# A two-layer diffusion block in split fp32 products: modulation sums, gates and an accumulator's first term moved between VectorE and ScalarE

## The chip, the cores and the metric

The kernel runs on one NeuronCore of a Trainium2 chip. A core has engines that run side by side, each with its own queue of instructions: TensorE (PE, the matrix products; its weight loads are shown apart as PEld), VectorE (DVE), ScalarE (ACT), GpSimd (POOL) and SyncE (SP, which starts transfers). They meet through semaphores. Matrix products leave their sums in PSUM, which VectorE and ScalarE can read and write; everything else lies in SBUF. The metric is the device time of one execution in microseconds (us), the median over runs.

## The reference

All is computed in fp32, on 256 latent tokens (`lat`) and 256 context tokens (`cx`) of width 1024. Layer 0 mixes by a short convolution, layer 1 by attention; after layer 1's mixer only the latent tokens are needed. Cut to what is computed here:

```python
def _rms(t, g):
    y = t * lax.rsqrt(jnp.mean(t * t, axis=-1, keepdims=True) + 1e-6)
    return y * g
def _modulate(t, g, shift, scale):
    return _rms(t, g) * (1 + scale) + shift
def _swiglu(h, w13, w2):                      # w13: 1024 x 5632, w2: 2816 x 1024
    gte, up = jnp.split(h @ w13, 2, axis=-1)
    return (jax.nn.silu(gte) * up) @ w2

for i in range(2):
    mod  = (silu(c)     @ mod_w[i] + mod_b[i]).reshape(bsz, 3, 3, 1, 1024)
    modc = (silu(c_ctx) @ mod_w[i] + mod_b[i]).reshape(3, 3, 1024)
    lat = lat + 0.5 * mod[:, 0, 2] * _swiglu(_modulate(lat, norm_g[i, 0], mod[:, 0, 0], mod[:, 0, 1]),
                                             ffn_w13[i, 0], ffn_w2[i, 0])
    cx  = ...                                 # the same with modc
    h, hc = _modulate(lat, norm_g[i, 1], ...), _modulate(cx, norm_g[i, 1], ...)
    y, yc = short_conv(h), short_conv(hc)     # i = 0: (b * dwconv3(c * x)) @ w_out
    y, yc = attention(h, hc), None            # i = 1: 8 query heads, 2 key heads, rope
    lat = lat + mod[:, 1, 2] * y
    if i == 0: cx = ...                       # mixer and second swiglu for cx too
    lat = lat + 0.5 * mod[:, 2, 2] * _swiglu(_modulate(lat, norm_g[i, 2], ...), ffn_w13[i, 1], ffn_w2[i, 1])
return lat
```

## The kernel before

**Products.** An fp32 product is three products of split operands: a high half (a ScalarE copy, L98) and the rest (a VectorE subtraction, L99), hi x hi + hi x lo + lo x hi (`mm3`, L118). Every weight is loaded raw (`wr`, three buffers of 128 x 2048), split (`split`, tiles `wh` and `wl`) and used. Names with h or l at the end (`gh`, `bl`, `th`) are such halves of activations. Tokens are the moving side: 256 (`S`, one stream) or 512 (`T2`, both).

**Swiglu.** `ffn(l, b, ...)` (L611) takes the 22 tiles of 128 hidden units in thirds of 8, 7 and 7. Each third makes its gated tiles g, and `project` (L462) multiplies them by w2 into 8 output tiles, which `finish` (L441) scales by the gate vector and adds to x, by one VectorE operation for each stream (L446). Most hidden tiles are computed by `Pair` (L539 on): the 2x2 block product (two halves of the model width by two streams, gate and up weights as the other side) in 7 products of half size in place of 8. A pair forms sums of weight blocks S1 to S4 (VectorE, into `ws`, L557 to L567), and uses sums T1 to T4 of the normed activations (`sums`, L320, one per normed block set). Its products are A11, A12, S1, S2, S4, S3, A22, twelve matmuls of 256 columns each, in two PSUM banks p and q. `head` does A11 into p and A12 into q's first half, `five` S1, `six` S2 and S4, `seven` S3, `four` A22; `seven` and `four` of a pair are placed among the next pair's products, or between the first products of `project`. The gate is copied out of p (L585, L595), added to q on VectorE (L597), and put through Silu (L598).

In ffn(0,0) tiles 3 to 7 of the first third are plain products. In ffn(0,1) and ffn(1,0) the first third starts with two plain tiles whose two streams are done one after the other, while the norm of the second stream is still being made; `Blocks.block` (L296) norms 4 x 256 columns at a time (VectorE products t with the rms factor, L256, ScalarE affine steps L305 and L310, then a split), and the T sums and the first pair's weight sums are made there too.

**Modulation.** The vectors `mod` are dot products of weight rows with silu(c): 224 units of one VectorE instruction each with an accumulated sum (`mod_unit`, L142) and a read-out of the accumulator. `tick(n)` (L179) spreads them over the program: a call adds n to what is owed, and each whole unit owed is issued. `mod_ready` (L186) issues the rest of a vector when it is needed.

**Attention and the last swiglu.** Heads are done in a loop: `scores` (L1033; maximum on VectorE, exponential on ScalarE, the scaling `pn` on POOL, L1058), `turn` (transposes, L1067, and a split) and `mix`. The last swiglu (from L1162, latent tokens only) does its first four tiles by `first_mm` on columns that need no norm yet (258 wide) and divides later (`first_post`, L1194). Tile 1 of them is followed by the norm of all 8 blocks of x: per block one VectorE product, one ScalarE high half (L1226) and one VectorE low half (L1227). The other tiles use matmuls of 512 and 256 columns (`mm2`, L1107).

**What sets the order.** The program is written in one order, and a scheduler places every instruction in its engine's queue by the dependencies it sees and its own estimate of when they are ready; an engine then runs its queue strictly in order. Six PSUM banks are shared by all products (`psum`, in rotation), two more serve small ones.

## Time and profile before

| | |
|---|---|
| median of 3 runs | 1587.94 us (1587.75 to 1588.68) |
| profiled execution | 1589.78 us, its span 1588.0 us |
| mean granted TensorE clock | 0.995 |
| TensorE busy | 1565.0 us, 99% |
| VectorE busy | 1319.8 us, 83% |
| ScalarE busy | 738.2 us, 46% |
| GpSimd busy | 29.8 us, 2% |
| read from HBM | 244.77 MB, 155 GB/s over the span |

Rows of the profile have the form "line engine operation output<-inputs, partitions x elements, x count". In a group's row the first number behind the bar is the busy time of the group in us, the next the mean of one in ns, and behind the second bar stands the idle time of the engine just before these instructions and what ended it. In a row of the timeline the first number is the start in us from the span's start, the second the busy time; an idle time before it stands in brackets. In a row of stretches the numbers are start and end, length, then busy time and instructions of PE, PEld, DVE, ACT and POOL, the granted clock of TensorE (1 is full speed), the busy share of the DMA engines, and GB/s. Matmuls overlap, so their pitch is read from start to start, not from the duration of one. A row of waits has "instruction <- releaser: us in total, times, longest us".

### The profile page before, as it was taken

The page shows a single profiled execution, that of the slowest core. Times are in us where ns is not written, and L with a number is a line of the kernel's source. Part 1 is how long each engine was busy: PE and PEld are TensorE (multiplying, and loading weights), DVE is VectorE, ACT ScalarE, POOL GpSimd, SP SyncE. Part 2 cuts the span into 40 slices and gives each one's busy share as a digit, 9 for nine tenths or more (in the row PEclk, how much of TensorE's full clock was granted, in tenths as well). Part 3 has the DMA queues.
Part 4 walks back from the last instruction along what each step waited for, and adds up shares of the span by engine and source line. Part 5 has one row for each costly group of instructions (what it writes and reads, how often), then busy time and mean ns, then how long its engine had stood idle before and what let it go on. Part 6 is the DMA issues. An engine that isn't in the chain of part 4 may idle for free.

```text
span 1588.0 us, 25040 instructions
## 1 busy us (share of the span) xinstructions
PE 1565.0 (99%) x10210; PEld 1423.9 (90%) x10210; DVE 1319.8 (83%) x2029; ACT 738.2 (46%) x1180; POOL 29.8 (2%) x20
## 2 busy tenths in 40 slices
PE   8999999999999999999999999999999999899998
PEld 6788998998888899989899899899899898888887
DVE  5778778879998879799798899898898899976654
ACT  5532452544322356335345375335255455655543
POOL 0000000000000000000000000000000005200000
PEclk9999999999999999999999999999999999999999
DMA  8545234234565412452342423443433654645552
GB/s 319 181 174 201 92 115 167 104 117 162 186 214 193 177 65 95 142 200 104 130 177 102 160 103 107 158 161 107 175 133 122 235 186 149 234 156 186 186 202 90
DMA packets 38419, 248.74 MB, mean 157 GB/s; under 512 B 5280, under 2 KB 7072, under 8 KB 11936
## 3 DMA queue, kind: packets, MB, share of 16 engines
q1 hardware_dynamic: 35712, 245.38, 43.5%
q10 hardware_dynamic: 2592, 1.76, 0.4%
q8 instruction: 80, 1.31, 0.3%
q14 instruction: 35, 0.29, 0.1%
HBM read 244.77 MB, written 1.05 MB: 155 GB/s over the span
## 4 chain that ended last, share of the span: by engine, by line
PE 93%; DVE 3%; ACT 2%; DMA 1%; issue 1%; POOL 0%; DVEq 0%; POOLq 0%; ACTq 0%
PE py L122 9%; PE py L123 9%; PE py L124 9%; PE p L124 7%; PE p L123 7%; PE p L122 7%; PE q L122 5%; PE q L123 5%; PE q L124 5%; PE py L1107 3%; PE pg L1107 2%; PE pu L1107 2%; PE pg L122 2%; PE pg L123 1%; PE pg L124 1%; PE pu L124 1%
## 5 line engine op out<-in xcount | busy, mean ns | idle before, releaser
L98 ACT ACTIVATE wh<-wr 128x1024 fp32r<-128x1024 f32 (+2 forms) x276 | 277.2, 1015 | 352.2 <-PE py L123 81.2
L99 DVE TENSOR_TENSOR wl<-wr,wh 128x1024 fp32r<-128x1024 f32 (+2 forms) x276 | 319.7, 1166 | 78.4 <-ACT wh L98 71.0
L142 DVE CUSTOM_DVE_ANT_0 junk<-wr,scbc,modb 128x1024 bf16<-128x1024 f32 x224 | 286.8, 1280 | 25.0 <-DMA wr<-in_modT 22.2
L123 PE MATMUL py<-gl,wh 128*128 128x512 f32 (+1 forms) x570 | 213.3, 374 | 0.0
L122 PE MATMUL py<-gh,wh 128*128 128x512 f32 (+1 forms) x570 | 213.3, 374 | 0.0
L124 PE MATMUL py<-gh,wl 128*128 128x512 f32 (+1 forms) x570 | 213.0, 374 | 0.0
L99 DVE TENSOR_TENSOR wl<-ws,wh 128x1024 fp32r<-128x1024 f32 x108 | 131.3, 1223 | 28.6 <-ACT wh L98 28.1
L98 ACT ACTIVATE wh<-ws 128x1024 fp32r<-128x1024 f32 x108 | 113.4, 1058 | 75.1 <-DVE ws L563 32.5
L124 PEld LDWEIGHTS py<-gh,wl 128*128 128x128 f32 x570 | 107.3, 188 | 19.1
L122 PEld LDWEIGHTS py<-gh,wh 128*128 128x128 f32 x570 | 107.4, 188 | 18.5
L123 PEld LDWEIGHTS py<-gl,wh 128*128 128x128 f32 x570 | 107.4, 188 | 18.2
L123 PE MATMUL p<-tl,wh 128*128 128x256 f32 x432 | 122.2, 283 | 0.0
L124 PE MATMUL p<-th,wl 128*128 128x256 f32 x432 | 122.2, 283 | 0.0
L122 PE MATMUL p<-th,wh 128*128 128x256 f32 x432 | 122.2, 283 | 0.0
L122 PE MATMUL q<-bh,wh 128*128 128x256 f32 x320 | 90.6, 283 | 0.0
L123 PE MATMUL q<-bl,wh 128*128 128x256 f32 x320 | 90.6, 283 | 0.0
L124 PE MATMUL q<-bh,wl 128*128 128x256 f32 x320 | 90.6, 283 | 0.0
L122 PEld LDWEIGHTS p<-th,wh 128*128 128x128 f32 x432 | 82.9, 192 | 0.3
L123 PEld LDWEIGHTS p<-tl,wh 128*128 128x128 f32 x432 | 82.9, 192 | 0.3
L124 PEld LDWEIGHTS p<-th,wl 128*128 128x128 f32 x432 | 82.9, 192 | 0.0
L446 DVE SCALAR_TENSOR_TENSOR x<-py,G,x 128x256 f32<-128x256 f32 x144 | 62.9, 477 | 6.3 <-PE py L124 6.0
L557 DVE TENSOR_TENSOR ws<-wr 128x1024 f32<-128x1024 f32 x54 | 65.7, 1218 | 0.0
(296 smaller groups left out, 4181.1 us busy)
## 6 DMA issues: line engine op xcount, KB each, us to landing
wr<-in_w SPq DMA_DIRECT2D x88, 1024.0 KB, 4.9
wr<-in_modT SPq DMA_DIRECT2D x64, 1024.0 KB, 4.8
wr<-in_w2b SPq DMA_DIRECT2D x24, 896.0 KB, 4.6
wr<-in_w2a SPq DMA_DIRECT2D x12, 1024.0 KB, 4.8
wr<-in_mod SPq DMA_DIRECT2D x8, 1024.0 KB, 6.1
wr<-in_cw_cx SPq DMA_DIRECT2D x8, 1024.0 KB, 4.8
wr<-in_w2l SPq DMA_DIRECT2D x8, 1024.0 KB, 4.8
wr<-in_cw_b SPq DMA_DIRECT2D x4, 1024.0 KB, 4.9
```

The lines of the kernel that those rows point to most:

```text
L98: nc.scalar.activation(out=hi, in_=src, func=AF.Copy)
L99: nc.vector.tensor_tensor(out=lo, in0=src, in1=hi.bitcast(F32), op=ALU.subtract)
L122: nc.tensor.matmul(ps, wh, mh, start=first, stop=False, **kw)
L123: nc.tensor.matmul(ps, wh, ml, start=False, stop=False, **kw)
L124: nc.tensor.matmul(ps, wl, mh, start=False, stop=last, **kw)
L142: nc.vector.tensor_tensor_reduce(out=junk, in0=raw[:, j * D : j * D + D], in1=scbc[:, v, :], scale=1.0, scalar=modb[:, l, col : col + 1], ...
L446: nc.vector.scalar_tensor_tensor(out=x[:, m, s * S : s * S + S], in0=ps[:, o : o + S], scalar=g[:, m, s : s + 1], in1=x[:, m, s * S : s * ...
L557: tt(out=sm.rearrange("p (a b c) -> p a b c", a=2, b=2)[:, :, 0, :], in0=a21.unsqueeze(1).to_broadcast([P, 2, T2]), in1=self.raw[:, T2 : 3 ...
L1107: nc.tensor.matmul(ps, w[0], m, start=first, stop=False, skip_group_check=True)
```

## The change

- *Modulation sums.* Where a vector is needed for both streams, the first stream's sum is made as before. For the second, VectorE multiplies the raw weights in place for a whole pair of blocks (2048 columns), and ScalarE sums them (`mod_both`, two activations with an accumulator). Such a unit counts 2 in `tick`; the amounts given to `tick` are changed in `ffn`, the convolution and attention, and one call is bound to an instruction of the pair before.
- *Gates.* `finish` of both streams scales by two ScalarE copies from PSUM and one VectorE addition of 512 columns.
- *Blocks.* A block of the norm is one VectorE product of 1024 columns and four ScalarE affine steps in place; the first block of a set (first stream, first half of the width) keeps the old form.
- *Pairs.* A11 goes to q's first half; ScalarE copies it to p, where S2 is added to it later, and A12 is added in q. So the first stream's gate is complete in q and needs no VectorE addition; its Silu is taken straight from PSUM, behind the copies. Weight sums are made in place in the raw buffer, for which A22 is split before them; the layout of w13 in memory is changed to fit. The raw buffers are four, `ws` is gone. The order of the products is A11, S3 of the pair before, A12, S1, A22 of the pair before, S2, S4.
- *PSUM.* The six banks are two rings of three.
- *Last swiglu.* Five early tiles, and the norm in two halves, behind tiles 2 and 3.

```diff
+FIRST = 5
...
-    psm = ctx.enter_context(tc.tile_pool(name="psm", bufs=6, space=bass.MemoryType.PSUM))
+    psm = ctx.enter_context(tc.tile_pool(name="psm", bufs=3, space=bass.MemoryType.PSUM))
...
+    turns = [0]
+
+    def psum(s="ps", side=None):
+
+        if side is None:
+            turns[0] += 1
+            side = "ab"[turns[0] % 2]
+        return psm.tile([P, T2], F32, tag=side, name=nm(s))
...
-        raw = wp.tile([P, 2048], F32, name=nm("wr"), tag="wr", bufs=3)
+        raw = wp.tile([P, 2048], F32, name=nm("wr"), tag="wr", bufs=4)
...
+    def mod_both(l, ch, pair, raw):
+
+        mt = mod_tile(l, ch)
+        r3 = raw.rearrange("p (j d) -> p j d", j=2)
+        nc.vector.tensor_tensor(
+            out=r3, in0=r3, in1=scbc[:, 1, :].unsqueeze(1).to_broadcast([P, 2, D]), op=ALU.mult
+        )
+        for j in range(2):
+            kt = pair * 2 + j
+            part = raw[:, j * D : j * D + D]
+            nc.scalar.activation(
+                out=part, in_=part, func=AF.Identity, accum_out=mt[:, kt, 1:2]
+            )
+        done[l, ch] += 2
+        if done[l, ch] == 16:
+            nc.vector.tensor_tensor(
+                out=mt[:, :, 1], in0=mt[:, :, 1], in1=modb[:, l, ch * KT : ch * KT + KT],
+                op=ALU.add,
+            )
...
-            units.extend(
-                (l, ch, pair, raw, j, v) for j in range(2) for v in range(streams(l, ch))
-            )
-        mod_unit(*units.pop(0))
-
-    def tick(n):
+            for j in range(2):
+                units.append((1, lambda j=j: mod_unit(l, ch, pair, raw, j, 0)))
+            if streams(l, ch) == 2:
+                units.append((2, lambda: mod_both(l, ch, pair, raw)))
+        weight, unit = units.pop(0)
+        unit()
+        return weight
+
+    def tick(n, behind=None):
 
         owed[0] += n
         while (jobs or units) and owed[0] >= 1:
-            owed[0] -= 1
-            next_unit()
+            if behind is None:
+                owed[0] -= next_unit()
+            else:
+                with tc.issue_after(behind.ins):
+                    owed[0] -= next_unit()
...
             raw = self.raw[hf, s] = hot("hr", F32)
             hi, lo = self.t["B", hf, s] = hot("bh"), hot("bl")
+            if not fine:
+                nc.vector.tensor_tensor(
+                    out=raw.rearrange("p (k t) -> p k t", k=4),
+                    in0=x[:, 4 * hf : 4 * hf + 4, s * S : s * S + S],
+                    in1=ri.unsqueeze(1).to_broadcast([P, 4, S]), op=ALU.mult,
+                )
             for i in range(4):
                 k = 4 * hf + i
                 c = slice(i * S, i * S + S)
+                b = B[:, k, s : s + 1]
+                if not fine:
+                    nc.scalar.activation(
+                        out=raw[:, c], in_=raw[:, c], func=AF.Identity,
+                        scale=A[:, k, s : s + 1], bias=b,
+                    )
+                    continue
...
         g = gate()
+        if c1 - c0 == T2:
+            t = tp.tile([P, T2], F32, name=nm("fy"), tag="gm", bufs=3)
+            for s in range(2):
+                c = slice(s * S, s * S + S)
+                nc.scalar.activation(
+                    out=t[:, c], in_=ps[:, c], func=AF.Identity, scale=g[:, m, s : s + 1]
+                )
+            nc.vector.tensor_tensor(out=x[:, m, :], in0=x[:, m, :], in1=t, op=ALU.add)
         for s in range(2):
-            if c0 <= s * S < c1:
-                o = s * S - c0
+            if c1 - c0 == S and c0 == s * S:
...
+    def w13_at(i, k):
+
+        return 1024 + (k + 4) % KT * P if i else k * P
+
     def w13_mm(pp, w, h, ks, c0, c1):
         for k in ks:
             mv = pick(h, k, c0, c1)
             for i in range(2):
-                mm3(pp[i][:, c0:c1], w((1 - i) * 1024 + k * P), mv, k == 0, k == KT - 1)
...
-            a21, a22, a11, a12 = (self.raw[:, i * T2 : i * T2 + T2] for i in range(4))
+            a11, a12, a22, a21 = (self.raw[:, i * T2 : i * T2 + T2] for i in range(4))
+            r4 = self.raw.rearrange("p (a c) -> p a c", a=4)
             tt = nc.vector.tensor_tensor
             if n == 0:
-                self.sm = sm = wp.tile([P, 2048], F32, name=nm("ws"), tag="ws", bufs=1)
+                self.w["A22"] = [
+                    wp.tile([P, T2], F32R, name=nm(t), tag=t, bufs=2) for t in ("w4h", "w4l")
+                ]
+                split(*self.w["A22"], a22)
                 tt(
-                    out=sm.rearrange("p (a b c) -> p a b c", a=2, b=2)[:, :, 0, :],
-                    in0=a21.unsqueeze(1).to_broadcast([P, 2, T2]),
-                    in1=self.raw[:, T2 : 3 * T2].rearrange("p (a c) -> p a c", a=2),
-                    op=ALU.subtract,
+                    out=r4[:, 0::3, :], in0=a21.unsqueeze(1).to_broadcast([P, 2, T2]),
+                    in1=r4[:, 0::2, :], op=ALU.subtract,
                 )
-                tt(out=sm[:, T2:1024], in0=a11, in1=sm[:, :T2], op=ALU.subtract)
-                self.keep(("S1", "S2"), sm[:, :1024])
+                tt(out=a22, in0=a22, in1=a11, op=ALU.subtract)
+                self.keep(("S2", "S1"), self.raw[:, 1024:])
                 return
-            sm = self.sm
-            tt(out=sm[:, 3 * T2 :], in0=a12, in1=sm[:, T2:1024], op=ALU.subtract)
-            self.keep(("S3", "S4"), sm[:, 1024:])
-            self.w["A22"] = [
-                wp.tile([P, T2], F32R, name=nm(t), tag=t, bufs=2) for t in ("w4h", "w4l")
-            ]
-            split(*self.w["A22"], a22)
+            tt(out=a12, in0=a12, in1=a22, op=ALU.subtract)
+            self.keep(("S3", "S4"), self.raw[:, :1024])
 
         def prod(self, ps, wk, hk, first=True):
             for k in range(4):
                 w = tuple(t[:, k * P : k * P + P] for t in self.w[wk])
                 mm3(ps, w, self.h.blk(hk, k), first and k == 0, k == 3, True)
 
-        def head(self):
-            p, q = psum("p"), psum("q")
-            self.p, self.q, self.q1 = p[:, :S], q, q[:, S:]
+        def one(self):
+            p, q = psum("p", "a"), psum("q", "b")
+            self.p, self.q0, self.q1 = p[:, :S], q[:, :S], q[:, S:]
             self.u = p
             self.sg = tp.tile([P, T2], F32, name=nm("sg"), tag="sg", bufs=3)
-            self.prod(self.p, "A11", ("B", 0, 0))
-            nc.scalar.copy(self.sg[:, :S], self.p)
-            self.prod(q[:, :S], "A12", ("B", 1, 0))
-
-        def five(self):
+            self.prod(self.q0, "A11", ("B", 0, 0))
+            nc.scalar.copy(self.p, self.q0)
+
+        def two_five(self):
+            self.prod(self.q0, "A12", ("B", 1, 0), False)
             self.prod(self.q1, "S1", "T1")
             self.gm = tp.tile([P, T2], F32, name=nm("gm"), tag="gm", bufs=3)
             nc.scalar.copy(self.gm[:, S:], self.q1)
+            nc.scalar.activation(out=self.sg[:, :S], in_=self.q0, func=AF.Silu)
 
         def six(self):
             self.prod(self.p, "S2", "T2", False)
-            nc.scalar.copy(self.sg[:, S:], self.p)
+            g = self.sg[:, S:]
+            nc.scalar.copy(g, self.p)
             self.prod(self.q1, "S4", ("B", 1, 1), False)
-            nc.vector.tensor_tensor(out=self.sg, in0=self.q, in1=self.sg, op=ALU.add)
-            nc.scalar.activation(out=self.sg, in_=self.sg, func=AF.Silu)
+            nc.vector.tensor_tensor(out=g, in0=self.q1, in1=g, op=ALU.add)
+            nc.scalar.activation(out=g, in_=g, func=AF.Silu)
 
         def seven(self):
             self.prod(self.p, "S3", "T3", False)
-            nc.vector.tensor_tensor(
+            return nc.vector.tensor_tensor(
                 out=self.u[:, S:], in0=self.p, in1=self.gm[:, S:], op=ALU.add
             )
 
...
             nc.vector.tensor_tensor(out=self.gm, in0=self.sg, in1=self.u, op=ALU.mult)
             split(g[0], g[1], self.gm)
 
-    def ffn(l, b, h, tot, gate, tail, gs=(), ev=1.5):
+    def ffn(l, b, h, tot, gate, tail, gs=(), ev=2):
...
                         pr.sums(1)
-                        pr.head()
-                    pr.five()
+                        pr.one()
                     if prev:
-                        prev.seven()
-                    pr.six()
+                        tick(0.5, prev.seven())
+                    pr.two_five()
                     if prev:
                         gs.append(new_pair("g"))
                         prev.four(gs[-1])
+                    pr.six()
...
             project(
                 ws2, lambda k, c0, c1: (cur[k][0][:, c0:c1], cur[k][1][:, c0:c1]), n,
-                gate, tail if end else None, tot, 2 if end and tot == T2 else 0, ev, between,
+                gate, tail if end else None, tot, 2 if end and tot == T2 else 0, ev - 0.5 * end, between,
...
-        tick(6)
+        tick(4.5)
...
-        tick(2)
+        tick(1)
...
+    def norm_half(hf):
+        u = hot("u", F32)
+        ks = slice(4 * hf, 4 * hf + 4)
+        nc.vector.tensor_tensor(
+            out=u.rearrange("p (k t) -> p k t", k=4), in0=x[:, ks, :S],
+            in1=ris.unsqueeze(1).to_broadcast([P, 4, S]), op=ALU.mult,
+        )
+        for q in range(2):
+            t = hot("h")
+            ht.append(t)
+            for j in range(2):
+                k = 4 * hf + 2 * q + j
+                c = slice((2 * q + j) * S, (2 * q + j) * S + S)
+                kw = {"scale": A[:, k, :1], "bias": B[:, k, :1]}
+                nc.scalar.activation(
+                    out=t[:, j * T2 : j * T2 + S], in_=u[:, c], func=AF.Identity, **kw
+                )
+                nc.scalar.activation(out=u[:, c], in_=u[:, c], func=AF.Identity, **kw)
+            h4 = t.rearrange("p (j h t) -> p j h t", j=2, h=2)
+            nc.vector.tensor_tensor(
+                out=h4[:, :, 1, :],
+                in0=u[:, q * T2 : q * T2 + T2].rearrange("p (j t) -> p j t", j=2),
+                in1=h4[:, :, 0, :].bitcast(F32), op=ALU.subtract,
+            )
...
-        if i < 4:
+        if i < FIRST:
...
+            if i in (2, 3):
+                norm_half(i - 2)
```

## The prediction

> **What bounds the kernel.** I read the page first (busy shares, then the chain that ended last), then busy time by stretches of the span, then what TensorE waited for, then the groups of instructions.

> ```profile
> span 1588.0 us, 25040 instructions
> PE 1565.0 (99%) x10210; PEld 1423.9 (90%) x10210; DVE 1319.8 (83%) x2029; ACT 738.2 (46%) x1180; POOL 29.8 (2%) x20
> PE 93%; DVE 3%; ACT 2%; DMA 1%; issue 1%; POOL 0%; DVEq 0%; POOLq 0%; ACTq 0%
> ```

> TensorE is busy 1565.0 of 1588.0 us and holds 93% of the chain. All idle time together is 23 us, so work taken off VectorE is worth something only where TensorE waits. The stretches show where that is (columns: stretch, length, PE, PEld, DVE, ACT, POOL busy, granted clock):

> ```profile
> 57.00:360.00 303.00, 303.00 (x1893) 275.08 (x1893) 247.68 (x346) 128.06 (x189) 0.00 (x0) 1.00 0.39 139
> 560.00:605.00 45.00, 43.68 (x352) 43.25 (x351) 34.91 (x52) 27.49 (x48) 0.00 (x0) 0.96 0.18 68
> 600.00:880.00 280.00, 280.00 (x2000) 265.14 (x2000) 248.38 (x339) 128.49 (x192) 0.00 (x0) 1.00 0.39 136
> 880.00:930.00 50.00, 49.25 (x302) 43.70 (x301) 45.38 (x86) 24.54 (x42) 0.00 (x0) 1.00 0.43 153
> 930.00:1240.00 310.00, 310.00 (x2224) 294.02 (x2223) 274.58 (x372) 144.96 (x215) 0.00 (x0) 1.00 0.38 136
> 1326.00:1368.00 42.00, 33.93 (x215) 28.68 (x214) 39.10 (x94) 24.66 (x58) 29.45 (x16) 0.96 0.42 152
> 1400.00:1425.00 25.00, 21.82 (x155) 20.87 (x155) 18.98 (x39) 14.67 (x31) 0.00 (x0) 0.93 0.34 126
> 1334.70:1338.10 3.40, 3.36 (x14) 3.03 (x15) 3.08 (x9) 2.71 (x6) 3.40 (x2) 0.56 0.02 2
> 1412.90:1416.30 3.40, 3.40 (x16) 3.31 (x17) 3.40 (x6) 0.42 (x1) 0.00 (x0) 0.60 0.20 31
> ```

> The three long stretches (893 us), where most of the edited code runs, have no idle TensorE at all: nothing can be won there, only lost. Idle time sits at the changes of stage, in attention (1326 to 1368, 8.07 us) and at the last swiglu (1400 to 1425, 3.18 us). The last two rows are the time just behind the two longest waits there: the clock is 0.56 and 0.60, which loses 1.5 and 1.4 us more of 3.4. The waits by releaser (total, times, longest):

> ```profile
> PE pg L1107 <- ACT wh L98: 3.2, 1, 3.2
> PE pt L1067 <- POOL pn L1058: 3.0, 3, 2.0
> PE py L124 <- DVE wl L99: 1.4, 1, 1.4
> PE pt L1067 <- DVE ptl L99: 1.4, 2, 1.0
> ```

> **Prices.** These are the groups of the moved work, with mean ns after the bar:

> ```profile
> L142 DVE CUSTOM_DVE_ANT_0 junk<-wr,scbc,modb 128x1024 bf16<-128x1024 f32 x224 | 286.8, 1280 | 25.0 <-DMA wr<-in_modT 22.2
> L142 DVE DVE_READ_ACCUMULATOR2_ANT mod<- 128x1 f32 x224 | 18.5, 82 | 0.0
> L446 DVE SCALAR_TENSOR_TENSOR x<-py,G,x 128x256 f32<-128x256 f32 x144 | 62.9, 477 | 6.3 <-PE py L124 6.0
> L98 ACT ACTIVATE wh<-ws 128x1024 fp32r<-128x1024 f32 x108 | 113.4, 1058 | 75.1 <-DVE ws L563 32.5 <-PE p L123 27.8 <-PE py L123 7.4
> L557 DVE TENSOR_TENSOR ws<-wr 128x1024 f32<-128x1024 f32 x54 | 65.7, 1218 | 0.0
> L563 DVE TENSOR_TENSOR ws<-wr,ws 128x512 f32<-128x512 f32 x54 | 37.0, 685 | 0.3
> L598 ACT ACTIVATE sg<-sg 128x512 f32<-128x512 f32 x54 | 33.6, 622 | 22.9 <-DVE sg L597 22.7 <-ACT w4h L98 0.2
> L595 ACT COPY sg<-p 128x256 f32<-128x256 f32 x54 | 19.6, 363 | 27.7 <-PE p L124 27.7
> L310 ACT ACTIVATE hr<-t,mod 128x256 f32<-128x256 f32 x32 | 14.6, 497 | 8.6 <-DVE t L256 8.5
> L142 DVE CUSTOM_DVE_ANT_0 junk<-wr,scbc,modb 128x1024 bf16<-128x1024 f32 x11 | 14.0, 1274 | 0.0
> ```

> *Modulation sums.* In the built kernel 96 of the 224 units on VectorE (1.28 + 0.08 us) become 48 products of 2048 columns (not in the trace; between 1.22, one L557, and 2.44, two; I take two) and 96 sums on ScalarE (1.06 each by the L98 row). VectorE: -96 x 1.36 + 48 x 2.44 = -14 us. ScalarE: +102 us, with 46% busy now. On the path nothing, under 57 to 360 and its like; without that cover it would be the 1.06.

> *Gates.* Two L446 per output tile become two scaled ScalarE copies (0.50 by L310) and one 512 add on VectorE (0.69): -0.27 us of VectorE per tile. With the other steps moved, the built kernel has 183 fewer 256-wide VectorE operations (0.48), 44 more of 512 (0.69) and 8 more of 1024 (1.22): -88 + 30 + 10 = -48. Together with the sums some 60 us, on the path nothing for the same reason.

> The seeded bank's rows, at the first pair of a third:

> ```profile
> 170.71 0.28 PE L124 MATMUL p<-hh,wl 128*128 128x256 f32 x1
> 170.83 0.28 PE L122 MATMUL q<-hh,wh 128*128 128x256 f32 x1
> 171.03 0.37 ACT L585 COPY sg<-p 128x256 f32<-128x256 f32 x1 [0.54 <-PE p L124]
> ```

> *The seeded bank, pairs in steady state.* A pair is 84 matmuls, started 0.12 us apart, 10.08 us. A11 now goes to q's first half, ScalarE copies it to p, and only then may A12 add to q. To cover that copy S3 of the pair before is put between. The longest new loop is the in-place sums: A22 must be split first (ScalarE 0.63, VectorE 0.69), then sum (0.69), low half of the previous gate (0.69), sum (0.69), then ScalarE: split 1.06, Silu 0.4 (between L595 and L310), copy 0.36. That is 5.2 us against four products, 48 x 0.12 = 5.76. Slack 0.5, so zero; without the slack 0.2 to 0.5 us for each of some 40 pairs.

> *First pair of the second and third thirds, six places.* No earlier pair is left to stand between A11 and A12.

> Before, A12 (q) starts 0.12 us behind A11 (p), and the copy behind it starts at +0.32. After, A12 waits for 0.20 (end to copy) + 0.36, less two matmuls that the built order puts there (0.24): 0.3 us; with a split (1.06) or a gate copy ahead of it on ScalarE, up to 1.0. I take 0.5, so +3 us (bounds +2 and +6).

> *Starts of ffn(0,1) and ffn(1,0).* Here normed blocks, T sums, two plain tiles and the first pair come close together. The rows of before at the first of them:

> ```profile
> 579.27 2.83 DVE L256 SCALAR_TENSOR_TENSOR t<-x,A,ss 128x256 f32<-128x256 f32 x7 [3.69 <-PE ss L248]
> 582.49 1.29 ACT L310 ACTIVATE hr<-t,mod 128x256 f32<-128x256 f32 x3
> 591.51 1.23 DVE L99 TENSOR_TENSOR wl<-wr,wh 128x1024 fp32r<-128x1024 f32 x1 [0.28 <-ACT wh L98]
> 590.42 1.06 ACT L98 ACTIVATE wh<-wr 128x1024 fp32r<-128x1024 f32 x1 [3.07 <-PE pg L123]
> 591.50 1.28 ACT L528 ACT_TABLE_LOAD   x1
> 594.75 1.05 ACT L98 ACTIVATE wh<-ws 128x1024 fp32r<-128x1024 f32 x1
> 606.73 2.36 DVE L99 TENSOR_TENSOR wl<-ws,wh 128x1024 fp32r<-128x1024 f32 x2 [0.59 <-ACT wh L98]
> 595.98 0.28 PE L124 MATMUL pu<-bh,wl 128*128 128x256 f32 x1
> 596.10 0.28 PE L122 MATMUL p<-bh,wh 128*128 128x256 f32 x1
> ```

> Before, the second norm's result comes at 579.27, the pair's weights are split at 590.42 and 591.51, and the pair starts at 596.10 without a wait. After, a block is one VectorE product (1.22), then four affine steps in place on ScalarE (0.40 apart), then the split: VectorE can no longer run beside them, since the sums need all four. I walked the built order from that result (time 0), by these rows' spacing (two 1024 products in 2.36, three affine steps in 1.29). VectorE product to 1.4, ScalarE affine to 3.05, high half 4.1 where TensorE wants it at 4.0; T sum 4.2, low half 5.4 (TensorE +0.7); second block 6.55, affine 8.2; sum 9.35, low half 10.5, then one more low half and two sums, 13.9. ScalarE's last T split ends 13.8, and behind it stand, in this order, the table load (15.1), Silu (15.7), and only then the pair's split (16.7, wanted 16.5) and its low half (17.9, TensorE +0.95). A11 and A12 last to 20.6; but the S sums lie between the gates on VectorE (to 20.85), a T split (21.85) and the S split (22.85) follow on ScalarE: +2.25. The low half comes at 24.9: +1.5. Sum 0.1 + 0.7 + 0.2 + 0.95 + 2.25 + 1.5 = 5.7 us, twice 11.4. Bounds: 0, as before; and 5.7 + 1.5 (clock after the longest wait) = 7.2, twice 14.4. I take the walk, since it is made of this place's own rows. Before's own losses at these places (1.32 idle, 4% of clock on 45 us = 1.8, and 0.75 at 880 to 930: 3.9) lie in front of it; the first blocks stay as they are, but less VectorE work stands ahead of them: -2 (0 to -3.9).

> How long an idle time must be before the clock drops decides the 1.5. The rows above show it after waits of 2.0 and 3.2 us, and the 2.25 lies there. [...]

> *Attention.* VectorE is busy 39.10 of 42 us. Of the 11 units there (1.36 us each with the read-out) five or six go, and three low halves of output weights (1.22) move in from the wait of 1.4 behind them: 6 x 1.36 - 3 x 1.22 = 4.5 us lighter, and that late wait goes too. The 2.0 behind POOL stays: POOL is busy 29.45 and nothing there is changed. -5 us (bounds -8 and -1).

> *Last swiglu.*

> ```profile
> 1405.52 1.30 ACT L1226 ACTIVATE h<-t,mod 128x256 fp32r<-128x256 f32 x3
> 1411.81 1.04 ACT L98 ACTIVATE wh<-wr 128x1024 fp32r<-128x1024 f32 x1
> ```

> The 3.18 wait and 1.4 of clock come from weights split (1411.81) behind 8 high halves on ScalarE. The new order norms four k at a time, behind tiles 2 and 3, and has one more early tile, which lends TensorE 48 x 0.12 = 5.8 us before it needs the norm. Against that ScalarE does two steps per k in place of one (8 x 0.40 = 3.2) and splits that tile's weights first (2 x 1.06): 3.18 + 3.2 + 2.1 - 5.8 = 2.7 us of wait, in pieces, so without the clock. -3.18 - 1.4 + 2.7 = -1.9 (bounds -4.6, no wait, and +2, all of the extra steps in the way and the clock as now). The fifth early tile has 48 matmuls of 258 columns for 32 of two widths: +0.2.

> *Start and the rest* (raw buffers 3 to 4, PSUM in two rings, retimed units): -0.3 (-1 to +1), hidden by TensorE's full stretches.

> Sum: 3 + 11.4 - 2 - 5 - 1.9 + 0.2 - 0.3 = +5.4, 1595.2 by the profiled execution, which took 1589.78 us. That is 1.84 above the median 1587.94, so 1593.3 in the median; I say 1593.

> **Rivals.** (a) *Faster, about 1582.* The waits at the two starts stay hidden, because the pair's split is taken as soon as tile 0's weights are free, as at 590.42. For it: before shows 3.4 us of room there (591.51 + 1.23 to 596.10). Against it: the order behind the table load. Then 5.4 - 11.4 = -6.0. It decides where the two starts together cost under 6.0 us; above that the change is not faster. (b) *A copy that stands in the way in steady state.* If the 5.2 us loop misses its 5.76, 40 pairs x 0.3 = +12 on top: 1605. For it: ScalarE takes 6.3 of 10.08 us per pair (three splits 3.2, two of half size 1.2, three copies 1.1, two Silu 0.8) and modulation sums of 1.06 queue in it. Against: a half-microsecond of slack and the extra raw buffer. (c) *Nothing moves, 1588.* TensorE's 1565 us stay and gains and losses cancel: the starts cost half of the walk. (d) ScalarE as the bound of the long stretches: 128 of 303 us now, and all that is added in the whole kernel would fit beside it; no chance of its own.

> **How the numbers follow.** A difference of 0.2% (3.2 us) is about what a measurement can tell from none. Forecast (slower by several us through the two starts): 0.45. (b) 0.08. (c) 0.12. (a) 0.35. The forecast's own range is 1591 to 1600 (bounds of the starts and attention). For 8 in 10 it reaches to (a) with attention and the last swiglu near their better ends, 1579, and to (b)'s lower half, 1604. Faster 0.35, same 0.12, slower 0.53.

> **What would show it.** Right: in the profile after, waits of TensorE for the pair's split (and its low half) near both starts, 4 to 6 us each; six short waits of q for the ScalarE copy; the three long stretches still without idle time; attention's idle from 8.07 to about 3; the 3.2 behind the split at the last swiglu in pieces. Wrong: full TensorE through both starts (a), or idle of 0.2 to 0.5 at each pair (b).

## The result, and the profile after

The changed kernel takes 1609.11 us (median of 4 runs, 1608.81 to 1610.19), the kernel before 1587.85 us beside it: a ratio of 1.0135, 95% interval 1.0117 to 1.0152. It is slower by 21 us where 5 were forecast, and lies above the forecast's range (1579 to 1604). The profiled execution took 1610.19 us.

The head of the page after, the two lines that answer to those of before:

```profile
span 1608.4 us, 25316 instructions
PE 1573.5 (98%) x10226; PEld 1428.8 (89%) x10226; DVE 1280.5 (80%) x1766; ACT 906.5 (56%) x1578; POOL 25.9 (2%) x20
```

VectorE is 39 us less busy, ScalarE 168 us more, and TensorE has 35 us in which it does nothing, where it had 23. It is also 8.5 us more busy with nearly the same matmuls (10226 for 10210).

**Where the time went.** To compare the two traces stage by stage, each was cut at the same amounts of TensorE work. The loss of a stage is the time from each matmul's start to the next one's, less what a packed matmul of its width takes (0.227 us at 512 columns, 0.120 at 256, 0.112 for the small ones, all from the traces), summed up. Single waits are given below by the same measure; the brackets of timeline rows and the tables of waits count from the modelled end of a matmul and are 0.1 to 0.2 us shorter (1.5 here is 1.3 there). In us:

| stage | before | after | difference | forecast |
|---|---|---|---|---|
| start-up, first 60 us of work | 20.9 | 21.8 | +0.9 | -0.3, "start and the rest" |
| pairs of ffn(0,0) | 0.1 | 1.3 | +1.1 | +1.0 |
| start of the convolution | 1.2 | 4.2 | +3.0 | in "the rest" |
| start of ffn(0,1) | 3.5 | 9.6 | +6.2 | +4.7 |
| pairs of ffn(0,1) | -0.1 | 2.5 | +2.5 | +1.0 |
| start of ffn(1,0) | 2.3 | 9.7 | +7.4 | +4.7 |
| pairs of ffn(1,0) | 0.0 | 2.6 | +2.6 | +1.0 |
| query, key and value projections | 6.0 | 7.7 | +1.6 | in "the rest" |
| attention | 8.2 | 5.1 | -3.1 | -5.0 |
| last swiglu | 5.2 | 3.2 | -2.0 | -1.7 |
| all, with the full stretches between (-0.3 in both) | 47.1 | 67.3 | +20.2 | +5.4 |

The two ends vary from execution to execution: in the profiles of this study the start-up row runs from 19.6 to 22.1 where the code there is that of before or of after, and all that follows the last swiglu's norm has lost 4.2 or 7.0 us. So 0.9 in the first row is no finding, and stages, not spans, are compared below.

Part of these losses is half clock. While products run, the records of the granted clock in the two profiles have it only in stretches of 3.41 us, in which matmuls of 256 columns start 0.213 us apart in place of 0.120: 16 of them, so 1.5 us lost for each stretch. Behind the start-up the changed kernel has three that the kernel before has not (at 394.5 in the start of the convolution, at 609.6 and 950.9 in the two starts) and lacks two that the kernel before has (573.9 and 1413.6). So some 1.5 of the 20.2 us is clock, and the rest is waits.

The same in the view of stretches. The first row is the start of the convolution in the kernel before. The others are of the changed kernel, in order of time: the start of the convolution, the start of ffn(0,1) and its last part, a long stretch of pairs, the start of ffn(1,0), a stretch of pairs, attention and the last swiglu:

```profile
360.00:430.00 70.00, 69.80 (x424) 62.35 (x423) 68.36 (x129) 30.47 (x48) 0.00 (x0) 1.00 0.45 158
...
360.00:430.00 70.00, 68.22 (x411) 61.50 (x410) 62.91 (x98) 40.51 (x74) 0.00 (x0) 0.98 0.44 156
580.00:612.00 32.00, 26.47 (x199) 25.04 (x199) 23.20 (x23) 17.82 (x26) 0.00 (x0) 0.96 0.10 34
604.00:609.50 5.50, 2.87 (x19) 2.46 (x20) 5.50 (x7) 2.52 (x3) 0.00 (x0) 1.00 0.00 0
...
617.00:897.00 280.00, 278.81 (x1973) 262.74 (x1972) 246.84 (x308) 165.16 (x284) 0.00 (x0) 1.00 0.41 143
940.00:975.00 35.00, 29.26 (x217) 27.64 (x217) 24.89 (x27) 18.86 (x27) 0.00 (x0) 0.95 0.09 29
988.00:1250.00 262.00, 260.82 (x1847) 245.93 (x1846) 226.16 (x286) 150.16 (x257) 0.00 (x0) 1.00 0.41 148
...
1351.00:1393.00 42.00, 35.77 (x236) 31.10 (x236) 34.95 (x85) 25.71 (x62) 25.72 (x16) 0.96 0.37 126
1422.00:1445.00 23.00, 21.11 (x168) 20.23 (x168) 17.85 (x29) 19.14 (x39) 0.00 (x0) 1.00 0.34 120
```

TensorE idles 5.5 and 5.7 us at the starts of ffn(0,1) and ffn(1,0), and over the whole of these stretches VectorE and ScalarE are not full either (23.20 and 17.82 of 32): for the most part the engines wait for one another. But VectorE is full in the last part of the first start, where TensorE idles most (5.50 of 5.50 us from 604.00). The stretches of pairs, full before, have 1.2 us of idle time each. The waits of TensorE:

```profile
PE q L129 <- ACT p L642: 3.8, 10, 0.6
PE q L131 <- DVE wl L106: 3.4, 3, 1.3
PE q L129 <- ACT wh L105: 3.2, 3, 1.3
PE pt L1126 <- POOL pn L1117: 3.1, 3, 1.5
...
PE pg L129 <- ACT bh L105: 2.4, 2, 1.9
PE pv L129 <- ACT hh L302: 1.8, 1, 1.8
...
PE pg L130 <- DVE bl L106: 1.1, 2, 0.6
```

All but POOL's row are new or, like the convolution's first high half (0.2 before), grown: q behind the ScalarE copy of the seeded bank (six first pairs, two in the middle of thirds, one at each start), the splits and low halves of the pair's weights and of the S sums at the starts, and the block's two halves there. The 3.2 us behind the split at the last swiglu is gone.

**The serial walk on the trace.** These are rows of the first start, VectorE and ScalarE above, TensorE below (start, busy time, idle time before it in brackets):

```profile
582.57 0.61 PE L284 MATMUL ss<-ident,ri 128*128 128x128 f32 x4
583.21 1.22 DVE L336 TENSOR_TENSOR hr<-x,ss 128x1024 f32<-128x1024 f32 x1 [2.40 <-PE ss L284]
584.47 2.08 ACT L346 ACTIVATE hr<-hr,mod,A 128x256 f32<-128x256 f32 x4 [4.93 <-DVE hr L336]
596.88 1.06 ACT L105 ACTIVATE th<-hr 128x1024 fp32r<-128x1024 f32 x1 [2.66 <-DVE hr L383]
597.97 1.28 ACT L588 ACT_TABLE_LOAD   x1
599.26 0.60 ACT L588 ACTIVATE sg<-pg 128x512 f32<-128x512 f32 x1
599.75 1.05 ACT L105 ACTIVATE wh<-wr 128x1024 fp32r<-128x1024 f32 x1
600.83 1.23 DVE L106 TENSOR_TENSOR wl<-wr,wh 128x1024 fp32r<-128x1024 f32 x1 [0.26 <-ACT wh L105]
600.85 0.39 PE L129 MATMUL q<-bh,wh 128*128 128x256 f32 x1 [0.56 <-ACT wh L105]
602.12 0.39 PE L131 MATMUL q<-bh,wl 128*128 128x256 f32 x1 [0.76 <-DVE wl L106]
604.00 0.39 PE L129 MATMUL q<-bh,wh 128*128 128x256 f32 x1 [0.45 <-ACT p L642]
607.01 0.38 PE L129 MATMUL q<-th,wh 128*128 128x256 f32 x1 [1.32 <-ACT wh L105]
609.06 0.39 PE L131 MATMUL q<-th,wl 128*128 128x256 f32 x1 [1.31 <-DVE wl L106]
```

With time 0 at 583.0, so that the first VectorE product ends where the walk has it: first VectorE product done at 1.4 (walk 1.4), affine steps 3.55 (3.05), last T split 14.9 (13.8), table load 16.2 (15.1), Silu 16.9 (15.7), pair's split 17.8 (16.7), its low half 19.1 (17.9). The order of the walk holds at every step. From the affine steps on it is late by half a microsecond, and from the second block's on by 1.1.

### The profile page after: what moved, and what is told of

Its sections match the earlier page's. It is cut to its first block, busy times and chain, and to the rows that moved or that the text cites. A ratio compares the mean times of both kernels' runs of the same rounds, so it can differ in the third digit from the quotient of the medians.

```text
span 1608.4 us, 25316 instructions
## 1 busy us (share of the span) xinstructions
PE 1573.5 (98%) x10226; PEld 1428.8 (89%) x10226; DVE 1280.5 (80%) x1766; ACT 906.5 (56%) x1578; POOL 25.9 (2%) x20
## 3 DMA queue, kind: packets, MB, share of 16 engines
HBM read 244.77 MB, written 1.05 MB: 153 GB/s over the span
## 5 line engine op out<-in xcount | busy, mean ns | idle before, releaser
L106 DVE TENSOR_TENSOR wl<-wr,wh 128x1024 fp32r<-128x1024 f32 (+2 forms) x384 | 448.2, 1183 | 133.6 <-ACT wh L105 126.1
L105 ACT ACTIVATE wh<-wr 128x1024 fp32r<-128x1024 f32 (+2 forms) x384 | 391.1, 1029 | 252.7 <-PE py L130 51.7
L149 DVE CUSTOM_DVE_ANT_0 junk<-wr,scbc,modb 128x1024 bf16<-128x1024 f32 x128 | 164.0, 1281 | 23.6 <-DMA wr<-in_modT 22.7
L129 PE MATMUL q<-bh,wh 128*128 128x256 f32 x480 | 137.3, 286 | 3.8 <-ACT p L642 3.3
L181 ACT ACTIVATE wr<-wr 128x1024 f32<-128x1024 f32 x96 | 101.1, 1056 | 64.9 <-DVE wr L175 43.8
L130 PE MATMUL q<-bl,wh 128*128 128x256 f32 x480 | 136.0, 283 | 0.0
L175 DVE TENSOR_TENSOR wr<-wr,scbc 128x2048 f32<-128x2048 f32 x48 | 109.8, 2288 | 0.7
L129 PEld LDWEIGHTS q<-bh,wh 128*128 128x128 f32 x480 | 92.1, 192 | 6.1 <-ACT p L642 4.9
L131 PEld LDWEIGHTS q<-bh,wl 128*128 128x128 f32 x480 | 91.8, 192 | 1.5 <-DVE wl L106 1.5
L130 PEld LDWEIGHTS q<-bl,wh 128*128 128x128 f32 x480 | 92.1, 192 | 0.2
```

The source lines that it names most:

```text
L105: nc.scalar.activation(out=hi, in_=src, func=AF.Copy)
L106: nc.vector.tensor_tensor(out=lo, in0=src, in1=hi.bitcast(F32), op=ALU.subtract)
L129: nc.tensor.matmul(ps, wh, mh, start=first, stop=False, **kw)
L130: nc.tensor.matmul(ps, wh, ml, start=False, stop=False, **kw)
L131: nc.tensor.matmul(ps, wl, mh, start=False, stop=last, **kw)
L149: nc.vector.tensor_tensor_reduce(out=junk, in0=raw[:, j * D : j * D + D], in1=scbc[:, v, :], scale=1.0, scalar=modb[:, l, col : col + 1], ...
```

## The experiments

Ratios are against the kernel before, timed beside each run. What a run does to a stage is read from its profile, as the loss defined above; "+" is against the kernel before. For the changed kernel the two starts are +6.2 and +7.4, together 13.6. A profile is of one execution, which can lie off the median (1609.47 for 1603.2 us in experiment 13, 1608.67 for 1604.5 in 5), and one stretch of half clock more or less is 1.5 us in a stage. So a difference of 1.5 us in one stage of one run is weak evidence, and where half clock makes the difference it is said.

**1. The old blocks in the changed kernel.**

```diff
         def block(self, s, hf, A, B, ri, fine=False):
-            if not fine:
-                nc.vector.tensor_tensor(out=raw..., in0=x[...], in1=ri..., op=ALU.mult)
...
-                    nc.scalar.activation(out=raw[:, c], in_=raw[:, c], func=AF.Identity, scale=A..., bias=b)
+                t = scaled(s, k, A, ri)
+                nc.scalar.activation(out=raw[:, c], in_=t, func=AF.Identity, bias=b)
```

> The changed kernel with the norm's blocks in their old form (VectorE products and ScalarE steps of 256 columns beside each other). Theory A, the serial block is what makes both starts late: the waits for the second block's halves (0.7 + 0.7 us at the first start, 2.0 + 0.7 and about 1.6 of clock at the second) go, and since all that follows starts some 2 us earlier, the waits for the pair's split go too: 10 to 15 us off, about 1596 us. Theory B, the in-place weight sums and the table load in front of Silu make the later waits: only the block waits go, 5 to 6 us off, about 1604, and waits of 1.5 us for the split of the S sums stay in the trace.

Measured: 1599.36 us, ratio 1.0066 (1.0045 to 1.0088). The starts are +2.9 and +1.6, 9.1 us less than in the changed kernel. The waits for the second block's high half are gone from the first start, and what is left there is mostly late copies and S sums (the rows are of the whole run):

```profile
PE q L129 <- ACT p L630: 4.0, 10, 0.6
PE q L129 <- ACT wh L105: 1.8, 3, 0.8
```

The size, 9.8 us off in all, is just short of theory A's 10 to 15. But of the S sums' waits 1.0 and 1.5 us stay at the first start, so B has a part too.

**2. The old pair in the changed kernel** (with three raw buffers, the buffer `ws`, the old layout of w13 and the old order of products; the half modulation unit that the changed kernel gives beside each pair goes with it).

```diff
-        def one(self):
...
-            self.prod(self.q0, "A11", ("B", 0, 0))
-            nc.scalar.copy(self.p, self.q0)
+        def head(self):
...
+            self.prod(self.p, "A11", ("B", 0, 0))
+            nc.scalar.copy(self.sg[:, :S], self.p)
+            self.prod(q[:, :S], "A12", ("B", 1, 0))
...
-                tt(out=a22, in0=a22, in1=a11, op=ALU.subtract)
+                tt(out=sm[:, T2:1024], in0=a11, in1=sm[:, :T2], op=ALU.subtract)
...
-                        tick(0.5, prev.seven())
+                        prev.seven()
```

> The changed kernel with the old pair (A11 into p, VectorE adds the gate, sums in a buffer of their own, three raw buffers, old layout of w13 and order of products). Theory B: the six waits behind A11 (0.4 to 0.6 each), two of 0.8 in the middle of thirds and at both starts the waits for the S sums' split (1.5 + 1.5) and for the copy (0.6) go: 5 + 7 = 12 us off, about 1597. Theory A: at the starts only the copy's wait goes, since the chain is late before it reaches the sums: 6 us off, about 1603.

Measured: 1597.06 us, ratio 1.0064 (1.0044 to 1.0084). The starts are +1.4 and +1.8, 10.4 us less. No wait for a ScalarE copy into p is left, and the loss at the start of the convolution is halved (+1.5): the waits there are those of before, and what is left is one stretch of half clock. One new wait of 1.9 us stands at the second third of ffn(0,1), for a low half of weights. Attention's gain is gone (8.2 us). The missing half units bear on that: 10 units stand in 42 us of attention here, where the kernel before has 11 and the changed one 4 or 5. So this run and experiment 7 are not the pair alone.

Each of the two runs takes away two thirds of the starts' loss. Neither theory holds alone. A reading that fits, with experiments 7 and 11, is that the block delays the chain, the in-place sums make it longer, and the slack in front of TensorE pays for only a part of the two.

**3. All modulation sums on VectorE in the changed kernel.**

```diff
             if streams(l, ch) == 2:
-                units.append((2, lambda: mod_both(l, ch, pair, raw)))
+                for j in range(2):
+                    units.append((1, lambda j=j: mod_unit(l, ch, pair, raw, j, 1)))
```

> The changed kernel with all modulation sums by VectorE, in the same places and counted the same. Theory: ScalarE's sums of 1.06 + 0.18 us stand in front of the first high half at the start of the convolution (wait 1.9, 3 us with what follows) and in front of the copy in the middle of two thirds (0.8 each): 3 to 5 us off, about 1605. Rival, VectorE needs the relief: the product of 2048 columns (2.29) and the read-outs cost it less than two sums (2.7), so VectorE gets 19 us more and waits for it appear in attention and at the starts: no gain or a loss, 1609 to 1613.

Measured: 1603.34 us, ratio 1.0098 (1.0078 to 1.0118). The two waits of 0.8 us in the middle of thirds are gone (their stage is 0.9 us better in ffn(0,1), 1.4 in ffn(1,0)). The start of the convolution is not better (+3.3): this half of the theory fell. The starts stay (+5.0 and +7.4; the first has no half clock here). Attention keeps its whole gain (-3.1), so that gain is not one of ScalarE's sums.

**4. The new last swiglu in the kernel before.**

```diff
-        if i < 4:
+        if i < 5:
...
-            if i == 1:
-                for q in range(4):
...
+            if i in (2, 3):
+                norm_half(i - 2)
```

> The kernel before with only the last swiglu of the changed one (five early tiles, norm in two halves). Theory: the wait of 3.2 us behind 8 high halves and 1.4 of clock go, smaller waits of 2.5 us come: 2 us off, about 1586. Rival: the gain of 2 us there in the changed kernel comes from attention ending differently before it: no difference, 1588.

Measured: 1585.02 us, ratio 0.998 (0.9971 to 0.999). The stage loses 2.7 us in place of 5.2, of which 1.4 is the half clock at 1413.6. This part is a gain by itself.

**5. The old gates in the changed kernel** (two VectorE operations from PSUM for each tile, `finish` as before).

> The changed kernel with the gates by VectorE (two operations of 256 columns from PSUM for each output tile). The run with the old modulation sums did not take the wait at the start of the convolution away, so they are not its cause. Theory: the gate's longer chain is (two ScalarE copies, one addition of 512, a square of 512, an addition of 512 before the norm's sum can be taken, and the square root's table loaded late behind them): 2 to 3 us off at the start of the convolution, and up to 1 at the query projections, about 1605. Rival: VectorE, 4 us in 100 busier at the end of each swiglu, is late with the same sum: no change there, 1608.

Measured: 1604.5 us, ratio 1.0101 (1.0075 to 1.0126). The start of the convolution is +2.5, down by 0.5 only, and that without half clock: the waits alone are 1 us longer than in the changed kernel. The projections (+2.0) and the starts (+6.2 and +7.5) are no better. The gates alone are not the cause.

**6. Silu's table loaded early.**

```diff
                 split(hi, lo, raw)
+                if s == 1 and hf == 0:
+                    w_ = tp.tile([P, 2], F32, name=nm("warm"), tag="rs")
+                    nc.scalar.activation(out=w_[:, :1], in_=hi[:, :1].bitcast(F32), func=AF.Silu)
```

> The changed kernel with one Silu of a single column put behind the high half of the second stream's first block, so that the table is loaded in a gap of ScalarE at both starts and not in front of the gates' Silu. Theory of the prediction, the serial walk: Silu, the pair's split and all behind them come 1.3 us earlier; at the first start the waits of 0.7 and 0.9 for the pair's split go and those for the S sums (1.5 and 1.5) shrink by about a microsecond in all, at the second the S sums' waits shrink likewise: 3 to 5 us off, about 1605. Rival: VectorE's own queue (13 operations of 1.2 us in a row) ends no earlier, so only the 0.7 goes: 1608.

Measured: 1606.99 us, ratio 1.0112 (1.0091 to 1.0132). The first start is 2.3 us better (+3.9): the 0.7 for the pair's split is gone and the 0.9 for its low half is 0.7. That is 0.8 us less of waits. The rest is the stretch of half clock, which does not come here although the waits of 0.6, 1.5 and 1.5 behind it stay as they were (rows in the last section). The second start is about 1 us worse, with waits 0.3 us shorter but two stretches of half clock in place of one. The table load is on the path in front of the pair's split, as the walk had it. The S sums do come 1.1 us earlier, counted from the block's VectorE product (22.7 us behind it for 23.8), which the rival denied, but TensorE also reaches them 1.1 us earlier, so their waits stay. VectorE has no gap there any more (3.42 of 3.42 us busy from 603.12, row in the last section).

**7. Both old, pair and blocks, in the changed kernel.**

> The changed kernel with both the old pair and the old blocks. Each alone took two thirds of the starts' loss away (9.1 and 10.4 of 13.6 us), more than all together, so the two share a slack. Theory: with both old nothing is left at the starts, within 1 us of before or better (the stretches of the starts), and what remains is the start of the convolution (+1.5) and the thirds' first pairs that the old pair showed with the new order of the modulation sums (+3.5 and 1.3): about 1591. Rival: the gates and modulation sums alone make the starts late: 2 to 3 us stay there.

Measured: 1593.06 us, ratio 1.003 (1.0016 to 1.0043). The starts are -1.9 and +1.0. The stretch that had 5.5 us of idle time:

```profile
580.00:612.00 32.00, 31.35 (x261) 31.10 (x260) 29.41 (x35) 22.14 (x33) 0.00 (x0) 1.00 0.26 94
```

So blocks and pair together are the cause of the starts' 13.6 us, and what the rest of the change does there is a gain of 1.9 us at the first (1.3 of it the half clock that the kernel before has at 573.9) and a loss of 1.0 at the second. What remains of the loss is elsewhere: +1.5 at the start of the convolution, +3.7 in the pairs of ffn(0,1), mostly the wait at the second third that experiment 2 has too and the half clock behind it, +1.4 in the pairs of ffn(1,0), and +1.5 in attention, all of it half clock; as in experiment 2 the gain there is gone.

**8. The kernel before with the new last swiglu and half the modulation units in attention.**

```diff
-    tick(2)
+    tick(1)
     k_rope(1, pk[1])
...
             mix(hd - 1, pts.pop(hd - 1))
-        tick(2)
+        tick(1)
```

> The kernel before with the last swiglu of the changed one and half as many modulation units in attention (one for two at each call). Theory: attention's gain of 3.1 us comes from fewer units on VectorE there, whoever sums them (it stayed whole in the run with all sums on VectorE): 2.5 at the last swiglu and 3 in attention off, about 1582. Rival: it comes from where the attention loop's steps happen to meet POOL's scaling (the old pair's run had the same units and no gain): 1585.

Measured: 1581.56 us, ratio 0.9956 (0.9942 to 0.9971): this version is faster than both kernels. Attention loses 4.1 us in place of 8.2, as the theory forecast. The rival's premise was wrong: the old pair's run did not have the same units (10 in 42 us). But the theory's reason is not shown either: VectorE is as busy here as before (39.74 us of 42 for 39.10), with 9 units for 11. The wait of 1.4 us for a low half of output weights is gone, and other waits for low halves are shorter, which points to the place of the units rather than their number. The stretch that held 8.07 us of idle TensorE, and the last swiglu's:

```profile
1326.00:1368.00 42.00, 37.65 (x246) 32.31 (x245) 39.74 (x93) 26.54 (x60) 29.17 (x16) 0.96 0.43 156
1400.00:1425.00 25.00, 22.77 (x176) 21.75 (x175) 19.77 (x32) 20.05 (x42) 0.00 (x0) 1.00 0.37 131
```

**9. Gates and modulation sums both old in the changed kernel** (3 and 5 together).

> The changed kernel with gates and modulation sums both by VectorE. Neither alone took the 3 us at the start of the convolution away. Theory: each alone leaves the norm's sum late, the one by the longer chain through ScalarE, the other by the long product on VectorE; with both old it is on time: 2 to 3 us less there than in the changed kernel, about 1602 in all. Rival: neither is the cause (the 512 wide accumulator, or the order in which the square root's table is loaded): the loss there stays above 2 us.

Measured: 1604.43 us, ratio 1.0102 (1.0078 to 1.0127). The start of the convolution is +0.5: the loss that neither took away alone is gone. The starts stay (+6.0 and +7.8). Of the convolution's gain 1.4 us is the half clock, which does not come there.

**10. One ring of six PSUM banks in the changed kernel.**

```diff
-    psm = ctx.enter_context(tc.tile_pool(name="psm", bufs=3, space=bass.MemoryType.PSUM))
+    psm = ctx.enter_context(tc.tile_pool(name="psm", bufs=6, space=bass.MemoryType.PSUM))
...
-        return psm.tile([P, T2], F32, tag=side, name=nm(s))
+        return psm.tile([P, T2], F32, tag="mm", name=nm(s))
```

> The changed kernel with its six PSUM banks as one ring. Theory: two rings of three are not what costs: within 1 us of the changed kernel in the stretches of the starts, 1608. Rival: products wait for a bank of their own ring while one of the other is free: the starts get 1 to 4 us better.

Measured: 1608.05 us, ratio 1.0127 (1.01 to 1.0153). The starts are +6.2 and +8.5. The rings cost nothing that shows here.

**11. The new blocks alone in the kernel before** (the edit of experiment 1 the other way).

> The kernel before with only the new blocks (one product of 1024, four steps in place). The walk has the second block's low half 1.4 us late and the pair's split then within before's 3.4 us of room. Theory: what is lost alone is the block's own waits, 1 to 2 us at each start, 1591; the rest of the starts' loss comes only together with the in-place sums. Rival: the block alone makes the whole chain late, as in the changed kernel with the old pair taken out: 5 us and more at each start, 1598.

Measured: 1595.7 us, ratio 1.0047 (1.003 to 1.0064). The starts are +2.9 and +5.3. At the second TensorE waits for the second block's high half, and the clock behind it is 0.57:

```profile
PE pg L122 <- ACT bh L98: 1.9, 1, 1.9
940.60:944.10 3.50, 2.98 (x13) 2.69 (x14) 2.52 (x3) 1.03 (x3) 0.00 (x0) 0.57 0.00 0
```

Both expectations missed: at the first start the loss is nearer to the theory, at the second it is the rival's. In the order of the instructions the second norm's result at the second start stands 36 matmuls (4.3 us) further down TensorE's queue than in the kernel before, as it does in the changed kernel, and in experiment 2 it stands 10 further up. With the old blocks in the changed kernel (experiment 1) it is back within one matmul of before, so there the new block moves it. So there is less work for TensorE behind it. The place alone is not enough: in experiment 14, with old blocks, the result stands 31 further down and this start loses 1.4 us more, not 5.3.

**12. A quarter of the units in attention's loop** (`tick(0.5)` in place of `tick(1)` in experiment 8).

> The kernel before with the new last swiglu and a quarter of the modulation units in attention's loop. Theory: VectorE is what attention waits for, and fewer units give more: 1 to 2 us below the run with half of them, 1580. Rival: POOL's scaling (29.6 us busy in 42) is the limit now, and the units that were not done come back behind attention: 1582 to 1584.

Measured: 1581.53 us, ratio 0.9962 (0.9944 to 0.9979); attention loses 4.1 us, as in 8. This decides nothing between theory and rival: in the two traces every engine runs the same instructions in the same order, so the smaller amount did not change the program, and the run is experiment 8 measured once more.

**13. The second norm asked for earlier in the changed kernel.**

```diff
-                    w13_mm(pp[0], w[0], h, range(KT), 0, S)
                     flush()
+                    w13_mm(pp[0], w[0], h, range(KT), 0, S)
```

> The changed kernel with the second stream's norm asked for before the first tile's products and not behind them: its result stands 22 and 21 matmuls (2.6 and 2.5 us) earlier in TensorE's queue at the two starts. Theory: the starts lose because the chain behind that result (17.9 us in the walk) is longer than the products that TensorE has left behind it; 2.5 us more of products take 2 to 2.5 us off each start, the 2.0 wait for the block's high half at the second start among it and its clock: 4 to 6 us off, about 1604. Rival: VectorE and ScalarE are late with the norm's own inputs at that place, so the result moves in the queue and not in time: 1608.

Measured: 1603.2 us, ratio 1.0101 (1.0076 to 1.0126). The starts are +3.7 and +6.0, 2.5 and 1.3 us better: at the second the 2.0 wait for the block is gone, but a wait of 0.7 for the pair's split has come. The result moves in time as well as in the queue, so the lack of products behind it is part of the cause. In this profile more than the gain is lost again: 4.0 us at the end of ffn(0,0), by a new wait of 2.3 for VectorE's sum in p and the half clock behind it, and 1.7 at the start of the convolution. The edit does not touch these places; why they are worse is open. The profile is of the slowest of the four executions (1609.47; the others took 1600.9 to 1603.9 us), so the gain in the median is not explained stage by stage.

**14. The new gates and modulation sums in the kernel before.**

> The kernel before with the new gates and the new modulation sums alone (old pairs, blocks, last swiglu and amounts of units). Theory: both together cost 2.5 to 3 us at the start of the convolution and 1 to 2 at the query projections, nothing in the full stretches: 1592. Rival: that loss needs the changed kernel's other timing of the units: 1588.

Measured: 1595.59 us, ratio 1.0046 (1.0033 to 1.0059). The start of the convolution is -0.1: the rival is right there, though the total missed both. The projections are +1.9, of which 1.5 is one more stretch of half clock (at 1279.9), the pairs of ffn(0,1) and ffn(1,0) +1.8 and +1.6, and the two starts -1.4 and +1.4.

## Why the prediction was wrong

The sign was right and its mechanism is the one measured: the serial block with the in-place sums at both starts. The size was not: 20.2 us of lost TensorE time where the sum had 5.4. The steps that failed are, by their share of the 14.8 us between: "start and the rest" (5.8, of which the start-up's 1.2 is no finding), the two starts (4.2), the pairs (3.2) and attention (1.9); the last swiglu came out 0.3 better. Step by step:

**What bounds the kernel.** Right. In the long stretches nothing was won by 39 us less of VectorE. (Some 60 had been forecast. The sums gave 21 for 14, the other steps 18 for 48; the sum of the forecast does not use it.) But "the path nothing" was not quite so for the modulation sums: the two new waits of 0.8 us in the middle of thirds come from ScalarE's queue, where the copy into p stands behind two splits, and these behind two of the modulation sums (from 765.57 on):

```profile
765.57 1.06 ACT L181 ACTIVATE wr<-wr 128x1024 f32<-128x1024 f32 x1 [1.67 <-DVE wr L175]
...
771.24 2.01 ACT L105 ACTIVATE wh<-wr 128x1024 fp32r<-128x1024 f32 x2 [0.18 <-DVE wr L625]
773.15 0.37 ACT L642 COPY p<-q 128x256 f32<-128x256 f32 x1
```

They cost 0.9 each by the stages, and experiment 3 takes them away. This is rival (b) in small: two pairs, not forty.

**First pairs of thirds.** Right: six waits of 0.4 to 0.5 us, 3.6 us with what follows them, for +3. The pairs' other 2.6 us are for the most part the two waits in the middle of thirds, put at nothing.

**The two starts.** The forecast for both was +9.4 us, and they measured +13.6. In front of the second norm's result they gained 3.3 us (-2 forecast): 2.6 at the first, of which 1.3 is the half clock that the kernel before has at 573.9, and 0.7 at the second. Behind it the trace has 17.1 us where the walk had 11.4 and its upper bound 14.4. Two things were wrong. First, the half clock was left out of the sum and only put into the range; it came at both starts and cost 3.0 us, all of that allowance. Second, the first wait, for the second block's high half, was put at 0.1 us and measured 0.7 at the first start and 2.0 at the second. The walk's other waits hold: 0.7 and 0.7 for the block's low half (0.7 in the walk), 0.7 and none for the pair's split (0.2), 0.9 and 0.25 for its low half (0.95), 0.6 for the copy and 1.5 for the S sums' split at each start (2.25 together), 1.5 and 1.5 for their low half (1.5).

Of the first wait a part is a price. The affine step has a scale and a bias for each partition, and was priced by a row with a bias alone:

```profile
L346 ACT ACTIVATE hr<-hr,mod,A 128x256 f32<-128x256 f32 x24 | 12.5, 590 | 15.6 <-DVE hr L336 15.6
L181 ACT ACTIVATION_READ_ACCUMULATOR wr<-wr 128x1 f32 x96 | 18.1, 188 | 0.0
```

It takes 0.59 us, 0.50 from start to start, where the walk had 0.40 (L310's 0.497 and its spacing): some 0.45 us for each of two blocks, most of the 1.1 that the walk is late by. And the step "twice" failed: the second start was not walked. Its second norm's result stands 36 matmuls further down TensorE's queue than before (13 at the first start), so less work is left to cover the block. Experiment 13 moves the result back by 2.5 us of products and takes the 2.0 us wait away. The table load, the third suspect, is on the path only to the pair's split (experiment 6).

**Attention.** Forecast -5, measured -3.1; TensorE's idle time in the 42 us went from 8.07 to 6.23, not to about 3. VectorE is lighter as forecast (34.95 us busy for 39.10; 4.5 lighter was the forecast), and the late wait of 1.4 us for a low half is gone as said. The waits behind POOL are not shorter (3.1 us in three against 3.0), and where the product with the values waited 1.1 us for a high half it now waits 1.1 for a low half. The step that failed is the price by VectorE's load: the load fell as forecast and the waits did not follow it, and experiment 8 gains 4.1 us with VectorE as busy as before. Which unit's place does it stays open.

**Last swiglu.** Forecast -1.7 with the fifth tile, measured -2.0, and -2.5 alone (experiment 4).

**"Start and the rest", -0.3 (-1 to +1).** This is the term that failed outright: the start of the convolution cost 3.0 us and the projections 1.6. They were put at nothing as "hidden by TensorE's full stretches", with no row of their own. At the start of the convolution 1.5 of the 3.0 are waits and 1.4 the half clock at 394.5, behind a wait of 1.8 us. Its rows:

```profile
386.72 1.28 ACT L516 ACT_TABLE_LOAD   x1
388.01 0.20 ACT L516 ACTIVATE ready<-acc 128x1 f32<-128x1 f32 x1
391.67 1.04 ACT L181 ACTIVATE wr<-wr 128x1024 f32<-128x1024 f32 x1
392.71 0.49 ACT L302 ACTIVATE hh<-t,mod 128x256 fp32r<-128x256 f32 x1
393.25 0.39 PE L129 MATMUL pv<-hh,wh 128*128 128x256 f32 x1 [1.78 <-ACT hh L302]
```

The square root's table is loaded late, behind the accumulator, and a modulation sum stands in front of the first high half. Which of the two counts is not settled by the runs: old gates leave +2.5, old modulation sums +3.3, both +0.5, and both new ones in the kernel before cost nothing there (-0.1). In experiments 2 and 7, too, with gates and sums new but the old pair and fewer units in ffn(0,0), the waits are those of before and only the half clock is left (+1.5). So the loss needs gates or sums and something else of the changed kernel, its amounts of units or its pair. Which unit it is that comes at the wrong moment stays open. So does the projections' loss: experiment 14 has +1.9 there, but 1.5 of it is half clock, and experiments 1, 10 and 13, which keep gates and sums, have +0.4, +0.1 and +0.2.

**The range.** The upper end took the other rival's lower half and the starts' bound, but no bound of a loss for the places that had been left in "the rest", and none for all terms erring on one side. Nearly all rows of the table above came out worse than forecast.

## What to carry to other kernels

In this kernel's long stretches, where TensorE is full, moving work from VectorE to ScalarE won nothing (39 us less and 168 more over the whole run), and the handovers that the move added (product, affine, split in place of steps side by side) were paid at the changes of stage, where the work behind a norm's result is short: 13.6 us at the two starts. Price every change of stage by itself, walk each one that the code shares, and read from the order of the instructions how much work the busy engine has left behind the result that all wait for. Before an experiment with smaller amounts is read, compare the order of the instructions with the run that it varies: here one such edit changed nothing. And count the stretches of half clock in each profile (1.5 us each here) before two of them are compared. The two parts that were worth keeping are those which took work from in front of a wait that the profile named: the last swiglu's norm and attention's units, 1581.6 us together.
